# Residual block kernel: first residual sum stored in the output tensor, second sub-layer added to it by accumulating DMAs

## The chip, the cores and the metric

The kernel runs on one core of a Trainium2 chip. The metric is the device time of one execution in microseconds (us), smaller is better. The kernel has five engines at its disposal: TensorE (PE, matrix products; its weight loads are listed as PEld), VectorE (DVE), ScalarE (ACT), GpSimd (POOL) and SyncE (SP). SP only issues transfers here. Transfers that POOL issues go through a queue of their own, which the profile calls software_dynamic; those of SP go through one called hardware_dynamic. Both queues are served by the same 16 DMA engines.

## The reference, cut to what matters

One layer over a sequence of 1024 tokens with 1024 channels, all float32. Only the last two lines of the first half and the last line concern the change: `x` after the first sub-layer is read twice, once by the normalisation ahead of the second sub-layer and once more by the final sum.

```
h = rmsnorm(x, pre_mix_g) * (1.0 + sc1) + sh1
y = hybrid_mixer(h, ...)                     # convolution branch + stick-breaking attention, gated, then w_o
x = x + ga1 * rmsnorm(y, post_mix_g)         # first residual sum
h = rmsnorm(x, pre_ffn_g) * (1.0 + sc2) + sh2
y = swiglu_ffn(h, w_ffn_in, w_ffn_out)       # (silu(gate) * up) @ w_ffn_out
return x + ga2 * rmsnorm(y, post_ffn_g)      # second residual sum, the output
```

## The kernel before, in words

Everything is kept transposed: a tile has 128 channels on the partitions and tokens along the row. The 1024 channels are 8 row blocks (`KT`), the 1024 tokens are two halves `c` of 512 (`CH`). The output in memory is `out[8, 128, 1024]`: row block, channel, token.

The kernel goes through the mixer, then the projection `w_o` with the first residual sum, then the first product of the second sub-layer (22 steps `f`, results stored to `g_d`), then the second product of the sub-layer (block from L1540 on). Each product of two float32 matrices is made of three passes with a high and a low part, and the larger ones are cut into seven block products instead of eight (Strassen's scheme), whose results are called `c11`, `c12`, `c21`, `c22`: the first digit is the half of the channels (row blocks 0 to 3 or 4 to 7) and the second the half of the tokens.

**First residual sum.** `res_add(c, n)` (L921) adds the block of `x` to the normalised `w_o` result on VectorE (L923), then stores the sum with a GpSimd transfer (`store`, helper L107) to a scratch tensor `x1_d[n]` in device memory (L924), then squares it on ScalarE for the next normalisation. There are 16 such stores, 128 rows of 2 KB each.

**Second product.** Three sweeps over 11 steps (`sweep`, names pa, pb, pc; matmuls at L1500), each step with weights that SP loads (`w2f` from `w_d`, helper L104), and then a last loop of 11 steps for the seventh block product, done in two halves of 256 tokens so that the first half can be finished while the second is multiplied. While it runs, `sum_sq` and `finish(1, 0)` finish tokens 512 to 1023; then, after the first half, `finish(0, 0)` finishes tokens 0 to 255; after the very last matmul, `finish(0, 1)` finishes tokens 256 to 511.

**finish(c, h, ps_sum, yy, last)** (L1624). From the channel sums of squares in PSUM it makes the reciprocal root (`rstd_from`: two ScalarE operations at L151 and L152, three on VectorE at L153 to L155). Then for four pairs `m` of row blocks: two multiplies by the reciprocal root (L1637 where the gain has been applied already, L1640 where it is applied in the same instruction), two adds of the first residual sum (the helper `add`, L1540 in the profile), and one store of the pair to `out` by SP (`load` is used for it, so that its line is L104). The pair is 128 partitions by two rows of 512 tokens (512 KB) for `c = 1` and by two rows of 256 tokens (256 KB) for each half of `c = 0`. That makes 12 stores.

**load_x1(c, alloc)** (L1647) brings the first residual sum back: eight transfers of 256 KB by SP for each half of the tokens, 16 in all, from `x1_d` into tiles `xr`: for `c = 1` into the pool `px` (four buffers, which the tiles of `c11` use before), for `c = 0` into four buffers of the pool `ops`, tag `op`, that the tiles `X` have used before.

**What sets the order.** Each engine and each queue executes its instructions in order. The framework's planner picks that order: it simulates the program with its own costs and takes, by priority, what is ready, so that transfers are issued well ahead of the loop in which they stand and the multiplies and adds of `finish` are not interleaved as they are written. Semaphores are set by the framework from the tiles that instructions share; `tc.add_manual_dep` adds an edge by hand.

Of the kernel before, what the change touches and what calls it, by code (L numbers as in the profile page):

```python
# [10 lines left out]
F32 = mybir.dt.float32  # L11
# [3 lines left out]
ALU = mybir.AluOpType  # L15
# [3 lines left out]
P = 128  # L19
D = 1024  # L20
T = 1024
KT = D // P
CH = 512
# [52 lines left out]
def tile_block(ctx: ExitStack, tc: tile.TileContext, xT, vecs, ada1, ada2, win, wv, wcv, wat, wo, w1, w2, cvw, out):  # L76
    nc = tc.nc
    act, dve, pool, pe = nc.scalar, nc.vector, nc.gpsimd, nc.tensor
# [6 lines left out]
    hp = mkpool(ctx, "hp", 16)  # L85
    dp = ctx.enter_context(tc.tile_pool(name="dp", bufs=1, space=DRAM))

    x1_d = [dp.tile([P, T], F32, name=f"x1_d{k}") for k in range(KT)]
    o_d = [dp.tile([P, T], F32, name=f"o_d{k}") for k in range(4)]
    v_d = [dp.tile([NG, P, TM], F32, name=f"v_d{k}") for k in range(CONVT)]  # L90
    u_d = [dp.tile([NG, P, TM], F32, name=f"u_d{k}") for k in range(CONVT)]
# [11 lines left out]
    def load(dst, src):  # L103
        return nc.sync.dma_start(dst, src)  # L104

    def store(dst, src):
        nc.gpsimd.dma_start(dst, src)  # L107
# [42 lines left out]
    def rstd_from(dst, m, a, ps_sum, n):  # L150
        act.activation(dst, ps_sum, AF.Abs_reciprocal_sqrt, bias=eps, scale=1.0 / n)  # L151
        act.activation(m, ps_sum, AF.Identity, bias=eps, scale=1.0 / n)  # L152
        dve.tensor_tensor(a, dst, dst, op=ALU.mult)  # L153
        dve.scalar_tensor_tensor(a, m, -0.5, a, op0=ALU.mult, op1=ALU.mult)
        dve.scalar_tensor_tensor(dst, a, 1.5, dst, op0=ALU.add, op1=ALU.mult)  # L155
# [47 lines left out]
    def bank(name):  # L203
        return psm.tile([P, CH], F32, tag="main", name=name)
# [428 lines left out]
    with ExitStack() as sG:  # L633
# [28 lines left out]
        for j in range(HK):  # L662
            f = [pg.tile([P, T], F32, tag="f", name=f"f{q}_{j}", bufs=2) for q in range(2)]
# [147 lines left out]
        for n in range(KT):  # L811
# [5 lines left out]
            y = yc[n]  # L817
# [35 lines left out]
    with ExitStack() as sF:  # L853
# [53 lines left out]
            pe.matmul(ps_sum, ones, src, start=True, stop=True)  # L907
            return ps_sum

        xrt = {}  # L910

        def xr_load(c):
            for n in range(0, KT, 2):
# [7 lines left out]
        def res_add(c, n):  # L921
            y, xr = h2[n, c], xrt[c, n // 2][:, n % 2]
            dve.tensor_tensor(y, y, xr, op=ALU.add)  # L923
            store(x1_d[n][:, c * CH:(c + 1) * CH], y)  # L924
            act.activation(xr, y, AF.Square)

        pairs_w = {}
# [193 lines left out]
        def a(n):  # L1121
            res_add(0, n)
# [96 lines left out]
        def a(n):  # L1219
            res_add(1, n)  # L1220
# [244 lines left out]
    with ExitStack() as sG:  # L1465
# [39 lines left out]
        def pull(n):  # L1505
            while todo and len(ahead) < n:
                fn, j = todo.popleft()
                ahead.append(fn(j))
# [30 lines left out]
        def add(eng, o, a, b):  # L1539
            eng.tensor_tensor(o, a, b, op=ALU.add)  # L1540
# [57 lines left out]
        def prep4(j, w):  # L1598
            return (wop2 if j < 6 else op2)(f"wa22_{j}", w[:, 0], act, dve)
# [5 lines left out]
        def out_tiles(nm, alloc):  # L1605
            for m in range(2):
                ytile[nm, m] = alloc[m](f"y{nm}_{m}")
            return [ytile[nm, n // 2][:, n % 2] for n in range(NH)]

        def sq_tile(name):  # L1610
            return po_.tile([P, CH], F32, tag="wt", name=name, bufs=3)

        def sum_sq(name, ys):
            acc = pg.tile([P, CH], F32, tag="acc", name=name, bufs=2)
            for n, y in enumerate(ys):
                if n == 0:
                    act.activation(acc, y, AF.Square)
                else:
                    sq = sq_tile(f"{name}_{n}")
                    act.activation(sq, y, AF.Square)  # L1620
                    add(dve, acc, acc, sq)
            return acc

        def finish(c, h, ps_sum, yy, last=None):  # L1624
            n = ps_sum.shape[-1]
            cols = slice(h * n, (h + 1) * n)
            dcols = slice(c * CH + h * n, c * CH + (h + 1) * n)
            rs = pg.tile([P, CH], F32, tag="rs", name=f"frs{c}{h}", bufs=2)[:, :n]
            m, a = (sq_tile(f"frs{c}{h}{i}")[:, :n] for i in "ma")
            rstd_from(rs, m, a, ps_sum, D)  # L1630
            for m in range(4):
                xr = xrs[c, m]
                y = ytile[yy[m // 2], m % 2]
                for i in range(2):
                    yi = y[:, i, cols]
                    if c == 0 and m < 2:
                        dve.tensor_tensor(yi, yi, rs, op=ALU.mult)  # L1637
                    else:
                        src = last[2 * (m - 2) + i][:, cols] if last else yi
                        dve.scalar_tensor_tensor(yi, src, gpost2[:, 2 * m + i:2 * m + i + 1], rs, op0=ALU.mult,  # L1640
                                                 op1=ALU.mult)
                    add(dve, yi, yi, xr[:, i, cols])
                load(out[2 * m:2 * m + 2, :, dcols].rearrange("n p t -> p n t"), y[:, :, cols])

        xrs = {}

        def load_x1(c, alloc):  # L1647
            for m in range(4):
                t = alloc(f"xr{c}_{m}")
                for i in range(2):  # L1650
                    load(t[:, i], x1_d[2 * m + i][:, c * CH:(c + 1) * CH])
                xrs[c, m] = t

        c11_d = dp.tile([P, NH, CH], F32, name="c11_d")
        c12 = out_tiles("c12", (h_tile, h_tile))
# [25 lines left out]
        def mmh(dst, h, n, j, w):  # L1681
            mm(dst, w, [t[:, h * W:(h + 1) * W] for t in T4[j]], n, False, j == FH - 1, True)

        A22 = []
        for j in range(FH):
            pull(1 + AHEAD)
            A22.append(prep4(j, ahead.popleft()))
            if j == FIN_AT[0]:
                load_x1(1, x_tile)
                ps1 = bank("fsum1")  # L1690
                pe.matmul(ps1, ones, sum_sq("acc1", c12 + c22), start=True, stop=True)
            if j == FIN_AT[1]:
                finish(1, 0, ps1, ("c12", "c22"))
            for n in range(NH):
                mmh(ka[n][:, :W], 0, n, j, A22[j])
        load_x1(0, g_tile)
        out_tiles("c11", (g_tile, g_tile))
        for m in range(2):
            load(ytile["c11", m], c11_d[:, 2 * m:2 * m + 2])
            for i in range(2):  # L1700
                y = ytile["c11", m][:, i]
                act.activation(y, y, AF.Copy, scale=gpost2[:, 2 * m + i:2 * m + i + 1])
        c21 = out_tiles("c21", (h_tile, h_tile))
        for h in range(2):
            cols = slice(h * W, (h + 1) * W)
            if h:
                for n in range(NH):
                    for j in range(FH):
                        mmh(ka[n][:, W:], 1, n, j, A22[j])
            ps0 = bank(f"fsum0{h}")[:, :W]  # L1710
            pe.matmul(ps0, ones, acc0[:, cols], start=True, stop=False)
            for n in range(NH):
                sq = sq_tile(f"fsq{h}_{n}")[:, :W]
                y = ka[n][:, cols]
                if h == 0:
                    y = c21[n][:, cols]
                    act.activation(y, ka[n][:, cols], AF.Copy)
                act.activation(sq, y, AF.Square)
                pe.matmul(ps0, ones, sq, start=False, stop=n == NH - 1)
            finish(0, h, ps0, ("c11", "c21"), ka if h else None)  # L1720
# [70 lines left out]
```

## Time and profile before

| | us |
|---|---|
| runs | 1421.28, 1414.62, 1413.15 |
| median | 1414.62 |
| span of the profiled execution | 1415.0 |
| PE busy in it | 1383.6 |
| DVE busy | 1060.4 |
| ACT busy | 651.3 |
| POOL busy | 96.7 |

The span is the time from the first to the last instruction of the one execution that the profiler recorded; it lies 0.4 us over the median of the runs. "Busy" is the time in which an engine executed something; issuing a transfer isn't counted. In the views below a row of a window gives its length, then for each engine its busy time with the number of instructions, then the TensorE clock granted (1 is full speed), the busy share of the 16 DMA engines and the GB/s moved. A row of the timeline gives start, duration, engine, line, operation and the tiles written and read. The chain of waits is the path that ended last, followed back from the end.

### The profile page before, as it was taken

Reading aid. Unit: us, or ns where it says so; the run is one execution under the profiler, and the core shown is the slowest. Engines: PE = TensorE matmul, PEld = TensorE weight load, DVE = VectorE, ACT = ScalarE, POOL = GpSimd, SP = SyncE. Lnnn points to the kernel's source line nnn. Section 1 sums busy time; section 2 is a strip of 40 time slices with the busy share of each in tenths; the row PEclk is TensorE's granted clock in tenths of the full one; section 3 lists DMA queues with packets and bytes.
Section 4 is the critical chain, followed back from the end, with each engine's and each line's share of the span. In section 5 each row is a group of like instructions: output and inputs, shape, how many; then the busy total and the mean of one; then the engine's idle time right before and its main releaser. Section 6 shows DMA issues by size and latency. Waiting matters only on the chain.

```text
span 1415.0 us, 18809 instructions
## 1 busy us (share of the span) xinstructions
PE 1383.6 (98%) x6886; PEld 1156.1 (82%) x6886; DVE 1060.4 (75%) x1602; ACT 651.3 (46%) x1136; POOL 96.7 (7%) x183
## 2 busy tenths in 40 slices
PE   7999999999999999999999999999999999999996
PEld 4798898898888878888877778888888887888886
DVE  6898598576767789779588878778877775775357
ACT  5375465364553447412356553334444453334441
POOL 0000000000001110000012100001111110000000
PEclk8999999999999999999999999999999999999998
DMA  9112041131253645784935545456777769588833
GB/s 382 74 37 75 30 141 54 45 114 66 77 177 111 228 179 175 280 277 137 361 120 173 185 147 173 157 173 228 242 255 246 259 245 392 170 333 280 281 116 119
DMA packets 91116, 258.73 MB, mean 183 GB/s; under 512 B 9744, under 2 KB 20112, under 8 KB 90000
## 3 DMA queue, kind: packets, MB, share of 16 engines
q1 hardware_dynamic: 75088, 202.99, 42.1%
q0 software_dynamic: 15936, 54.54, 10.3%
q8 instruction: 54, 0.88, 0.3%
q14 instruction: 38, 0.31, 0.1%
HBM read 190.91 MB, written 66.58 MB: 182 GB/s over the span
## 4 chain that ended last, share of the span: by engine, by line
PE 80%; DVE 6%; issue 6%; DMA 5%; ACT 2%; POOL 1%; SPq 0%; DVEq 0%; POOLq 0%; ACTq 0%
PE ka L958 12%; PE ka L1500 8%; PE kc L958 7%; PE pwo L881 6%; PE pb L1500 4%; PE pgv L180 3%; PE pg L180 3%; PE pyc L180 3%; PE pya L180 3%; PE pv L481 3%; PE pcv L461 3%; PE tr L571 2%; PE pq L180 2%; PE pgg L180 2%; PE pk L180 2%
## 5 line engine op out<-in xcount | busy, mean ns | idle before, releaser
L559 DVE TENSOR_TENSOR_SCAN ka<-ka 128x128 f32<-128x128 f32 (+2 forms) x96 | 91.4, 968 | 22.8 <-ACT ka L555 22.5
L555 ACT ACTIVATE ka<-z 128x128 f32<-128x128 f32 (+2 forms) x96 | 47.1, 496 | 58.8 <-PE z L554 34.4
L575 DVE TENSOR_TENSOR alo<-tr,ahi 128x512 fp32r<-128x512 f32 x80 | 53.2, 685 | 18.2 <-ACT ahi L574 17.5
L1500 PE MATMUL ka<-gt,w2f 128*128 128x512 f32 x264 | 63.4, 390 | 0.8 <-DMA w2f<-w_d 0.8
L574 ACT ACTIVATE ahi<-tr 128x512 fp32r<-128x512 f32 x80 | 46.3, 601 | 38.1 <-PE tr L571 25.8
L561 DVE TENSOR_TENSOR be<-be,ka 128x127 f32<-128x127 f32 (+2 forms) x96 | 53.4, 573 | 9.6 <-ACT be L556 4.9
L1500 PEld LDWEIGHTS ka<-gt,w2f 128*128 128x128 f32 x264 | 49.4, 188 | 11.5 <-issue 1.4
L1066 PE MATMUL ke<-b,w_hi 128*128 128x512 f32 x176 | 55.2, 394 | 0.0
L135 DVE SCALAR_TENSOR_TENSOR ada<-ada,cb 128x1024 f32<-128x1024 f32 x32 | 38.8, 1223 | 20.7 <-DMA ada<-in_ada_dram 20.6
L556 ACT ACTIVATE be<-z 128x128 f32<-128x128 f32 (+2 forms) x96 | 46.2, 495 | 9.5 <-PE tr L571 9.3
L571 PE MATMUL tr<-ident,be 128*128 128x128 f32 x288 | 47.8, 273 | 0.4 <-DVE alo L575 0.4
L580 PE MATMUL av<-ahi,vst 128*128 128x256 f32 x160 | 44.2, 292 | 0.0
L461 PE MATMUL pcv<-ph,cvw 128*128 128x128 f32 x320 | 42.5, 276 | 0.8 <-DMA ph<-v_d 0.8
L581 PE MATMUL av<-alo,vst 128*128 128x256 f32 x160 | 42.8, 293 | 0.0
L461 PEld LDWEIGHTS pcv<-ph,cvw 128*128 128x128 f32 x320 | 39.5, 192 | 1.5 <-issue 1.2
L1066 PEld LDWEIGHTS ke<-b,w_hi 128*128 128x128 f32 x176 | 33.0, 188 | 7.8 <-issue 1.0
L481 PE MATMUL pv<-wv_hi,hhi 128*128 128x256 f32 x128 | 36.8, 288 | 2.1 <-DVE qst L505 1.4
L159 ACT ACTIVATE gt<-X 128x512 fp32r<-128x512 f32 x33 | 20.4, 630 | 39.5 <-DVE X L1543 12.4
L481 PE MATMUL pv<-wv_hi,hlo 128*128 128x256 f32 x128 | 36.7, 287 | 0.0
L481 PE MATMUL pv<-wv_lo,hhi 128*128 128x256 f32 x128 | 36.4, 285 | 0.0
L551 PE MATMUL z<-kst,qst 128*128 128x256 f32 (+2 forms) x96 | 36.2, 382 | 0.0
L571 PEld LDWEIGHTS tr<-ident,be 128*128 128x128 f32 x288 | 34.7, 140 | 1.8 <-PE z L554 0.5
(533 smaller groups left out, 4097.7 us busy)
## 6 DMA issues: line engine op xcount, KB each, us to landing
w_d<-w2o POOLq DMA_DIRECT2D x44, 512.0 KB, 8.0
w2f<-w_d SPq DMA_DIRECT2D x44, 512.0 KB, 5.4
ada<-in_ada_dram SPq DMA_DIRECT2D x32, 512.0 KB, 6.1
w2r<-in_w_dram SPq DMA_DIRECT2D x44, 256.0 KB, 3.8
w1g<-in_w_dram SPq DMA_DIRECT2D x21, 512.0 KB, 3.6
w1u<-in_w_dram SPq DMA_DIRECT2D x21, 512.0 KB, 5.2
cvw<-in_cvw_dram SPq DMA_DIRECT2D x20, 512.0 KB, 3.7
ada_w<-in_ada_dram SPq DMA_DIRECT2D x8, 1024.0 KB, 12.0
```

The source lines that it names most:

```text
L180: pe.matmul(bank, st[:, cols], mv[k][:, c * CH:(c + 1) * CH], start=(i == 0 and s == 0), stop=(i == n - 1 and s == 2))
L461: pe.matmul(cv[:, gi * TM:(gi + 1) * TM], wts[n][:, at:at + P], ph[:, g, SH - 1 - d:SH - 1 - d + TM], start=(d == 0), stop=(d == SH - 1))
L481: pe.matmul(pv[:, :256], st[k][:, tcols], mv[:, wc], start=(k == 0 and i == 0), stop=(k == KT - 1 and i == 2))
L555: act.activation(kap[:, s_lo:s_hi], z[:, zo:zo + w], AF.Sigmoid, bias=0.0, scale=-0.125)
L559: dve.tensor_tensor_scan(rev, rev, rev, init, op0=ALU.mult, op1=ALU.bypass)
L561: dve.tensor_tensor(beta[:, :m], beta[:, :m], kap[:, s_lo + 1:s_lo + 1 + m], op=ALU.mult)
L571: pe.transpose(tr[:, o:o + P], src, ident)
L575: dve.tensor_tensor(alo, tr, ahi, op=ALU.subtract)
L881: pe.matmul(bank_, st[:, cols], mv[k][:, cs], start=(k == 0 and q == 0), stop=(k == KT - 1 and q == 2))
L958: pe.matmul(bank_, st[:, cols], t[:, mv], start=(first and j == 0 and s == 0), stop=(j == HK - 1 and s == 2), skip_group_check=not first)
L1066: pe.matmul(kbs[f], wes[f][st][:, cols], t[:, mv], start=(i == 0 and j == 0 and q == 0), stop=(j == HK - 1 and q == 2), skip_group_check=i ...
L1500: pe.matmul(dst, w[st][:, cols], g[mv], start=first and s == 0, stop=last and s == 2, skip_group_check=more)
```

## The change

The scratch tensor `x1_d` is gone. `res_add` stores the first residual sum into `out`, at the place of the final result, still with a GpSimd transfer, and keeps a handle on it. `finish` no longer adds on VectorE; each pair of scaled row blocks is sent to `out` by a GpSimd transfer with `accum_op=ALU.add`, which adds to what lies in memory. By hand, each of the 12 accumulating transfers is made to depend on the two stores that wrote its place. `load_x1`, its two calls and the tiles `xr` of this block are gone.

```
-    x1_d = [dp.tile([P, T], F32, name=f"x1_d{k}") for k in range(KT)]
...
-        xrt = {}
+        xrt, x1_st = {}, {}
...
         def res_add(c, n):
             y, xr = h2[n, c], xrt[c, n // 2][:, n % 2]
             dve.tensor_tensor(y, y, xr, op=ALU.add)
-            store(x1_d[n][:, c * CH:(c + 1) * CH], y)
+            x1_st[c, n] = nc.gpsimd.dma_start(out[n, :, c * CH:(c + 1) * CH], y)
             act.activation(xr, y, AF.Square)
...
             for m in range(4):
-                xr = xrs[c, m]
                 y = ytile[yy[m // 2], m % 2]
                 for i in range(2):
                     yi = y[:, i, cols]
...
                         dve.scalar_tensor_tensor(yi, src, gpost2[:, 2 * m + i:2 * m + i + 1], rs, op0=ALU.mult,
                                                  op1=ALU.mult)
-                    add(dve, yi, yi, xr[:, i, cols])
-                load(out[2 * m:2 * m + 2, :, dcols].rearrange("n p t -> p n t"), y[:, :, cols])
-
-        xrs = {}
-
-        def load_x1(c, alloc):
-            for m in range(4):
-                t = alloc(f"xr{c}_{m}")
+                acc = nc.gpsimd.dma_start(out[2 * m:2 * m + 2, :, dcols].rearrange("n p t -> p n t"),
+                                          y[:, :, cols], accum_op=ALU.add)
                 for i in range(2):
-                    load(t[:, i], x1_d[2 * m + i][:, c * CH:(c + 1) * CH])
-                xrs[c, m] = t
+                    tc.add_manual_dep(acc.ins, x1_st[c, 2 * m + i].ins.name,
+                                      mybir.DependencyInfo(mybir.DependencyClass.Sync, mybir.DependencyReason.DATA))
...
             if j == FIN_AT[0]:
-                load_x1(1, x_tile)
...
-        load_x1(0, g_tile)
```

## The prediction

> **What bounds the kernel now.** I read the page first, then the windows of the last stage, then the chain of waits at its end. The page says who is full:
>
> ```profile
> span 1415.0 us, 18809 instructions
> PE 1383.6 (98%) x6886; PEld 1156.1 (82%) x6886; DVE 1060.4 (75%) x1602; ACT 651.3 (46%) x1136; POOL 96.7 (7%) x183
> PE   7999999999999999999999999999999999999996
> ```
>
> PE is busy for 1383.6 of 1415.0 us; the slices show the rest at the two ends. DVE is busy for 75%, but what it does beside a full PE costs nothing. So I ask of each edit whether it sits where PE has run dry. The windows of the second product, and what PE waits for in them (window 1200 to 1420):
>
> ```profile
> 1200.00:1250.00 50.00, 50.00 (x222) 41.40 (x222) 37.11 (x59) 21.72 (x39) 0.00 (x0) 1.00 0.57 192
> 1250.00:1300.00 50.00, 49.25 (x217) 40.26 (x216) 33.84 (x54) 12.98 (x22) 0.00 (x0) 1.00 0.93 349
> 1300.00:1350.00 50.00, 50.00 (x222) 41.42 (x221) 20.34 (x30) 24.75 (x42) 0.00 (x0) 1.00 0.77 256
> 1350.00:1380.00 30.00, 30.00 (x181) 26.60 (x180) 18.02 (x28) 14.15 (x23) 0.00 (x0) 1.00 0.31 100
> 1380.00:1390.00 10.00, 10.00 (x78) 9.71 (x77) 9.65 (x15) 3.35 (x10) 0.00 (x0) 1.00 0.00 1
> 1390.00:1402.00 12.00, 12.00 (x101) 11.97 (x100) 9.52 (x24) 1.89 (x5) 0.00 (x0) 1.00 0.73 263
> 1402.00:1415.00 13.00, 1.83 (x9) 1.27 (x8) 6.96 (x19) 1.22 (x3) 0.00 (x0) 0.68 0.24 81
> ...
> PE ka L1500 <- DMA w2f<-w_d: 0.8, 1, 0.8
> ```
>
> The first number after the length is PE's busy time. It equals the length everywhere but in two rows: 0.75 us are missing between 1250 and 1300, the one wait of PE, for a weight; and PE does 1.83 of the last 13 us. Only these two places can give time. The chain of waits of the last one:
>
> ```profile
> 1402.10 1.74 PE fsum L1719 x8
> ...
> 1403.87 0.48 ACT frs L151
> ...
> 1405.83 1.43 DVE yc L1637 x4
> 1407.26 1.57 DVE yc L1640 x4
> 1408.83 0.33 DVE yc L1540
> 1409.16 0.34 DVEq L1786
> 1409.50 2.01 DVE yc L1540 x6
> ```
>
> After the last matmul come the reciprocal root (to 1405.83), eight multiplies (to 1408.83), eight adds (to 1411.51) and the last store. The planner has put all multiplies ahead of all adds.
>
> **The change part by part.**
>
> *First sums stored to `out`.* 16 GpSimd stores before, 16 after, same tiles and row lengths, on the same queue. Zero; they lie around 718 to 776, beside a PE that has other work.
>
> *16 loads of the first sum, gone.* They are on SP's queue, between the weights. The chain of waits at the one gap of PE:
>
> ```profile
> 1245.82 0.44 SPq L104
> ...
> 1246.80 8.66 DMA xr<-x_d
> ...
> 1255.52 10.40 DMA w2f<-w_d
> 1265.92 0.14 issue
> 1266.05 2.99 PE ka L1500 x12
> ```
>
> By this chain it is the landing of an `xr` load, after 8.66 us, that lets SP go on at 1255.5, and the weight that it issues then lands 10.40 us later, in a window whose DMA engines are 0.93 busy. Without the eight loads of `c = 1` (2 MB) that weight comes earlier by more than 0.75 us, so the wait goes: -0.75 us, at most. The least it can be is zero, if the planner fills the room with other early loads. I take -0.75. Next to be late is nothing that the rows show: every other row of the stage is full. The eight loads of `c = 0` lie in 1300 to 1350, where PE waits for nothing: zero.
>
> *24 adds, gone.* Three groups of eight on DVE:
>
> ```profile
> 1382.42 5.39 DVE L1640 SCALAR_TENSOR_TENSOR yc<-yc,gpost,frs 128x512 f32<-128x512 f32 x8
> 1387.73 4.90 DVE L1540 TENSOR_TENSOR yc<-yc,xr 128x512 f32<-128x512 f32 x8
> ...
> 1396.93 2.77 DVE L1540 TENSOR_TENSOR yc<-yc,xr 128x256 f32<-128x256 f32 x8
> ```
>
> The first 4.90 and the second 2.77 us run under PE: zero. The last eight, from 1408.83 to 1411.51, are on the path: the last transfer's data are ready 2.68 us earlier.
>
> *12 stores by SP become 12 accumulating transfers by POOL.* What is behind them on POOL: nothing, its last record in the trace is a store at 1185.88. Each also waits for two stores of the first sums, which were issued some 600 us before: zero. What they cost is the way to the first byte, the data and the landing. Before:
>
> ```profile
> 1185.88 0.54 POOL L107 DMA_DIRECT2D g_d<-p  x1 [0.78 <-DVE p L1394]
> ...
> 1409.53 2.38 SPq L104 DMA_DIRECT2D out_dram<-yc  x4
> ...
> 1409.53:1410.30 0.77, 0.00 (x0) 0.00 (x0) 0.77 (x3) 0.00 (x0) 0.00 (x0) 0.50 0.00 0
> 1410.30:1413.80 3.50, 0.00 (x0) 0.00 (x0) 1.21 (x4) 0.00 (x0) 0.00 (x0) 0.50 0.87 300
> 1413.80:1415.00 1.20, 0.00 (x0) 0.00 (x0) 0.00 (x0) 0.00 (x0) 0.00 (x0) 0.50 0.00 0
> ```
>
> SP issues the first of the last four at 1409.53 and no byte moves for 0.77 us; then the 16 engines are busy for 0.87 x 3.50 = 3.05 us with the megabyte; 1.20 us after it the span ends. For POOL the nearest rows are the stores of the first sums around 718: the whole group by line, landing times in the window 715 to 735, and the windows behind the first issue, which started at 718.36:
>
> ```profile
> L107 POOL DMA_DIRECT2D x_d<-y x16 | 8.7, 542 | 143.1 <-DVE y L923 142.9
> ...
> x_d<-y POOLq DMA_DIRECT2D x8, 256.0 KB, 2.3
> ...
> 718.36:719.10 0.74, 0.74 (x5) 0.62 (x4) 0.74 (x2) 0.36 (x1) 0.54 (x1) 1.00 0.00 0
> 719.10:719.40 0.30, 0.30 (x3) 0.23 (x2) 0.30 (x2) 0.10 (x1) 0.00 (x0) 1.00 0.00 0
> 719.40:719.70 0.30, 0.30 (x3) 0.26 (x2) 0.30 (x1) 0.30 (x1) 0.14 (x1) 1.00 0.91 355
> ```
>
> An issue takes POOL 0.54 us, the first byte moves 1.04 us after its start, and 256 KB land after 2.3 us. An accumulate has 256 rows where these have 128, so an issue may take up to 1.08 us. The pairs become ready at 1406.55, 1407.26, 1408.04 and 1408.83, about 0.76 us apart; at 1.08 us each the last issue would start at 1406.55 + 3 x 1.08 = 1409.79. That is before the data of the earlier ones are through in what follows, so it costs nothing.
>
> The unknown is how long the data of an accumulate occupy the engines: call it k times the 3.05 us of a megabyte's plain store. Below, k = 1: the add is free. Then the last issue decides, 1408.83 + 2.3 = 1411.13, and with 1.20 us behind it the span would end at 1412.3, 2.7 us earlier. That is the gain's limit. Above there is no row; but an accumulate must read the old megabyte as well as write the new one, which before was a load and a store, so k = 2 is what the bytes ask for if nothing is overlapped. I take k = 2, the nearest to rows of this kernel: data from 1406.55 + 1.04 = 1407.59 for 6.1 us to 1413.69, and 1.20 us to the end at 1414.9. Against 1415.0 that is -0.1 us: what the adds give, the second reading takes.
>
> The Trainium skill (Collectives: The Full Stack, section The bandwidth ceiling: the fold count and why AG ≠ RS ≠ AR) has the add itself as free and says that its cost is the second source read on the same ring, 32.35 against 62.28 GB/s. By that, 1.93 x 3.05 = 5.9 us, an end at 1414.7 as an estimate from that page; no run here shows it yet.
>
> *Sum.* 1415.0 - 0.75 - 0.1 = 1414.15 for the profiled execution. Its span stands 0.4 us over the median of the runs, so 1413.8 us. With k = 1 it is 1412.3 - 0.75 - 0.4 = 1411.15.
>
> **The rivals.** About 0.5% of this kernel, 7.1 us, is what a measurement can tell from no change.
>
> *Slower: the accumulates back up.* The twelve move 4 MB, 12.2 us of plain data, and the first pair is ready after two of the eight multiplies at 1382.42, at 1383.77, its first byte moves at 1384.8. If k is large, the engines never run dry from there and the end is 1384.8 + 12.2 k + 1.2. This passes the forecast's way of reckoning at k = 2.5; k = 3 gives 1422.6, less 0.75 and 0.4 is 1421.4; k = 4 gives 1433.6. From about k = 3 on it is over 0.5% slower. For it: rows of 1 KB and 2 KB, each with a read, a read and a write, and nothing in the trace that shows such a transfer. Against: the plain store of the same rows runs at 300 GB/s in its window, and k = 3 asks for more than the bytes do.
>
> *Each accumulate waits for the one before to land,* if the framework sees one tensor written twice. A landing is 2.3 us and another 0.76 of data: 1406.55 + 4 x 3.06 + 1.20 = 1420.0, less 0.75 and 0.4 is 1418.8. With landings over 3.8 us it would pass 0.5%. Against: the 12 stores before go to the same tensor and four were issued within 2.38 us.
>
> *The adds weren't what ended last, or the change frees more than I see.* The multiplies would end at 1408.83 in any case; to be faster by 7.1 us over half of the 13 us behind the last matmul would have to go, or a gap of PE that the windows don't show. No row speaks for it, except that the planner orders the stage anew.
>
> **How the numbers follow.** Forecast, k from 1 to 2.5: 0.70, at 1411 to 1416. k from 2.5 to 3: 0.06, up to 1421, still within 0.5%. k over 3: 0.15, slower. One after the other: 0.05, of which 0.03 within 0.5% and 0.02 slower. Faster by an order that I don't see: 0.04. So faster 0.04, same 0.70 + 0.06 + 0.03 = 0.79, slower 0.15 + 0.02 = 0.17. The range goes from 1411, the free add, to 1425, k = 3.3, which leaves out about 0.16 in all.
>
> **What would show it.** Right: no `xr` load in the second product, the wait at 1266 gone, PE full until its last matmul about 0.75 us earlier; the first of the last four accumulates issued by POOL some 0.8 us after the first multiply of `finish(0, 1)` starts; about 6 us of busy DMA engines behind it. Step by step wrong: an issue over 1.1 us on POOL (the issue would bound the tail), busy DMA engines without a break from 1385 to the end (backlog), POOL waiting for a transfer between accumulates (one after the other), a new wait of PE in the sweeps (the planner). A time under 1407.5 or over 1421.7 would make the forecast wrong.

## The result, and the profile after

The changed kernel took 1420.12 us in the median of ten runs (1417.39 to 1423.29), the kernel before 1414.49 us in the ten runs beside them: a ratio of 1.0032, 95% interval 1.002 to 1.0045. By this ratio it became slower by some 4.5 us (the two medians lie 5.6 us apart, within the interval's 2.8 to 6.4). No change was forecast, with a time 0.8 us under the median then known. The difference lies within the 0.5% that was called no change, but it is clear of the noise and has the other sign.

The profiled execution after the change has a span of 1416.8 us. First the page, then the windows of the second product that answer to those of before (same columns: PE, PEld, DVE, ACT, POOL, clock, DMA share, GB/s):

```profile
span 1416.8 us, 18768 instructions
PE 1383.9 (98%) x6886; PEld 1157.1 (82%) x6886; DVE 1051.1 (74%) x1578; ACT 651.2 (46%) x1136; POOL 111.0 (8%) x195
```
```profile
1250.00:1300.00 50.00, 50.00 (x222) 41.39 (x222) 32.05 (x51) 14.49 (x25) 0.00 (x0) 1.00 0.81 288
1300.00:1350.00 50.00, 50.00 (x222) 41.40 (x221) 20.12 (x30) 22.08 (x38) 0.00 (x0) 1.00 0.68 223
...
1380.00:1390.00 10.00, 10.00 (x76) 9.68 (x76) 6.74 (x14) 2.92 (x9) 4.82 (x4) 1.00 0.84 130
1390.00:1402.00 12.00, 10.33 (x80) 9.77 (x78) 2.86 (x8) 1.99 (x5) 4.83 (x4) 1.00 0.93 155
1402.00:1417.00 15.00, 0.00 (x0) 0.00 (x0) 3.29 (x9) 0.00 (x0) 4.86 (x4) 0.52 0.53 70
```

PE is full from 1250 on, the gap at 1266 is gone, and it is through with its work before 1402. Two numbers from here on measure every kernel: the **sweeps**, from the first matmul of the second product to the end of the last matmul of all, and the **tail**, from there to the end of the span. The start of the sweeps is the first start time in the next two rows (this line's matmuls, before and after), the end is the last matmul's row in the timeline (1398.44 + 1.89 = 1400.33; before, 1403.83):

```profile
L1500 PE MATMUL ka<-gb,wa x132: 389/389/497, 1186.1 to 1243.1; 128*128 128x512 f32 x132
```
```profile
L1499 PE MATMUL ka<-gb,wa x132: 389/389/499, 1183.7 to 1240.8; 128*128 128x512 f32 x132
```
```profile
1398.44 1.89 PE L1709 MATMUL fsum<-fsq,ones 128*128 128x256 f32 x8
```

The sweeps went from 217.7 to 216.6 us, 1.1 us less. The tail went from 11.2 to 16.5 us, 5.3 us more. The sum, +4.2 us, is what the runs show; that the sweeps begin 2.4 us earlier in this execution is left out of it, since in the executions of the kernels below they begin anywhere from 1183.7 to 1189.7.

Where the tail went: the accumulates on POOL and the last multiplies in the timeline, the transfers of the window 1404 to 1417, and the windows in which the last megabyte moves and after it.

```profile
1402.33 1.43 DVE L1635 TENSOR_TENSOR yc<-yc,frs 128x256 f32<-128x256 f32 x4
1403.39 4.86 POOL L1640 DMA_DIRECT2D out_dram<-yc  x4 [8.40 <-DVE yc L1635]
1403.68 1.65 DVE L1638 SCALAR_TENSOR_TENSOR yc<-ka,gpost,frs 128x256 f32<-128x256 f32 x4
```
```profile
DMA packets 1088, 1.05 MB, mean 81 GB/s; under 512 B 64, under 2 KB 1088, under 8 KB 1088
...
q0 software_dynamic: 1088, 1.05, 61.5%
...
out_dram<-yc POOLq DMA_DIRECT2D x4, 256.0 KB, 6.2
```
```profile
1404.90:1412.90 8.00, 0.00 (x0) 0.00 (x0) 0.43 (x2) 0.00 (x0) 3.35 (x3) 0.50 1.00 131
1412.90:1416.80 3.90, 0.00 (x0) 0.00 (x0) 0.00 (x0) 0.00 (x0) 0.00 (x0) 0.50 0.00 0
```

The adds are gone, and the data are ready at 1405.3. But the 16 DMA engines are full for 8.0 us (61.5% of 13 us) with the megabyte that took them 3.05 us, and when the last byte has moved, at 1412.8, there are 4.0 us in which no engine computes and no byte moves. Before there were 1.4. What the second stretch is, the waits of SP at the very end tell, before and after:

```profile
SPq L1786 <- DMA out_dram<-yc: 1.7, 3, 0.7
SPq L1786 <- PEq L1786: 0.6, 2, 0.5
```
```profile
SPq L1776 <- DMA out_dram<-yc: 43.6, 2, 42.3
SPq L1776 <- PEq L1776: 2.9, 2, 2.5
```

The first row of each is the wait for the output to land. The second is the closing barrier, where all engines meet: SP stood there for up to 2.5 us instead of 0.5. The page's name PEq is only who came last by its reckoning. The records of the trace themselves (start in us, duration, engine, operation) name the one who was late:

```
after    1405.60  10.43  GpSimd  DRAIN
         1405.62   2.62  GpSimd  DMA_DIRECT2D out_dram<-yc   (the last accumulate)
         1413.76   0.01  Sync    DRAIN                        (SP is at the barrier)
         1416.08   0.02  GpSimd  EVENT_SEMAPHORE              (GpSimd is at the barrier)
before   1185.86   8.43  GpSimd  DRAIN
         1185.88   0.54  GpSimd  DMA_DIRECT2D g_d<-p          (its last transfer)
         1414.29   0.01  Sync    DRAIN
         1414.32   0.02  GpSimd  EVENT_SEMAPHORE
```

The last instruction of GpSimd's own program is a drain. Before, it began at 1186 and nobody saw it. Now it begins behind the last accumulate and ends 3.2 us after the last byte, 2.3 us after SP has seen everything land.

### The profile page after: what moved, and what is told of

It is laid out like the page before. It is cut to its first block, busy times and chain, and to the rows that moved or that the text cites. A ratio compares the mean times of both kernels' runs of the same rounds, so it can differ in the third digit from the quotient of the medians.

```text
span 1416.8 us, 18768 instructions
## 1 busy us (share of the span) xinstructions
PE 1383.9 (98%) x6886; PEld 1157.1 (82%) x6886; DVE 1051.1 (74%) x1578; ACT 651.2 (46%) x1136; POOL 111.0 (8%) x195
## 4 chain that ended last, share of the span: by engine, by line
PE 87%; issue 4%; DVE 3%; DMA 2%; ACT 2%; POOL 1%; POOLq 0%; SPq 0%; DVEq 0%; ACTq 0%
PE ka L957 14%; PE kc L957 8%; PE ka L1499 8%; PE pwo L880 6%; PE pb L1499 4%; PE pgv L179 3%; PE pyc L179 3%; PE pg L179 3%; PE pya L179 3%; PE pv L480 3%; PE pcv L460 3%; PE ka L414 2%; PE tr L570 2%; PE pq L179 2%; PE pgg L179 2%
## 5 line engine op out<-in xcount | busy, mean ns | idle before, releaser
L158 ACT ACTIVATE s1o<-s 128x512 fp32r<-128x512 f32 x22 | 13.8, 629 | 49.7 <-PE ka L957 41.6
```

## The experiments

Two theories were set against each other: A, that the end is tied to GpSimd's drain, and B, that it is tied to the longer data time of the accumulates. A table first; the numbers of each row are from the profiled execution of that kernel, the ratio is to the kernel before on the same chip. "Last byte" is counted from the end of the last matmul, "behind it" from there to the end of the span.

| kernel | sweeps | last byte | behind it | tail | ratio (95%) |
|---|---|---|---|---|---|
| before | 217.7 | 9.8 | 1.4 | 11.2 | 1 |
| after | 216.6 | 12.5 | 4.0 | 16.5 | 1.0032 (1.002 to 1.0045) |
| e1_plain_pool | 216.6 | 8.0 | 4.6 | 12.6 | 1.001 (0.9996 to 1.0024) |
| e2_sp_no_add | 216.6 | 6.9 | 1.4 | 8.3 | 0.9973 (0.996 to 0.9985) |
| e3_one_pool_store | 217.5 | 10.2 | 4.2 | 14.4 | 1.0035 (1.0022 to 1.0048) |
| e4_half | 217.3 | 9.8 | 1.7 | 11.5 | 0.9996 (0.9983 to 1.0008) |
| e6_three_quarters | 216.9 | 10.2 | 1.4 | 11.6 | 1.0001 (0.9989 to 1.0012) |
| e7_split_adds | 216.6 | 10.8 | 2.5 | 13.3 | 1.0016 (1.0004 to 1.0028) |
| e8_tiny_pool | 217.4 | 10.0 | 4.2 | 14.2 | 1.0025 (1.0007 to 1.0043) |
| e9_loads_on_pool | 216.6 | 10.4 | 2.5 | 12.9 | 1.001 (0.9995 to 1.0024) |
| e10_loads_only | 216.6 | 9.8 | 1.4 | 11.2 | 1.0002 (0.9989 to 1.0015) |
| e11_tiny_compute | 217.8 | 9.8 | 3.8 | 13.5 | 1.0014 (1.0 to 1.0028) |

**e1_plain_pool.** From the changed kernel, with the scratch tensor back:

```
-                acc = nc.gpsimd.dma_start(out[...], y[:, :, cols], accum_op=ALU.add)
+                store(out[...], y[:, :, cols])
```

> The changed kernel with plain GpSimd stores in place of the accumulating ones (the first residual sum is left out of the output). Theory A: the end is set by GpSimd's closing drain, which in the changed kernel ends 7.8 us after the end of the last transfer's issue on that engine. Then the end stays tied to that issue: the stretch from the last matmul's end to the end of the span is 14.0 us (if a plain issue takes 0.54 us) to 16.5 us (if it takes 1.2 us), where the changed kernel has 16.5 and the kernel before 11.2. Rival B: the longer data time of the accumulates (7.3 us for the last megabyte against 3.05) sets it. Then the stretch falls to 8.6 us: multiplies, a landing of 2.5 us and the closing.

```profile
1407.60 2.96 POOL L107 DMA_DIRECT2D out_dram<-yc  x4 [10.39 <-DVE yc L1636]
```
```profile
DMA packets 321, 1.06 MB, mean 92 GB/s; under 512 B 64, under 2 KB 64, under 8 KB 320
...
q0 software_dynamic: 320, 1.05, 26.7%
...
out_dram<-yc POOLq DMA_DIRECT2D x4, 256.0 KB, 2.9
```

The first fence is the timeline of POOL, the second the transfers from 1406.5 to 1418. Neither theory got its number: 12.6 us of tail lies between 8.6 and 14.0. The drain ended 5.8 us behind the last issue, not 7.8, so A in its first form fell; but it ended 3.8 us behind the last byte, where the changed kernel has 3.2. Both costs are real then. From e2_sp_no_add to this kernel the queue alone is exchanged: 4.3 us more tail, 1.1 until the last byte and 3.1 behind it. From this kernel to the changed one the add alone is put in: 3.9 us more, 4.5 until the last byte and 0.6 less behind it. The plain store goes out in 256 packets of 4 KB beside 64 small ones (320 in all), the accumulate in 1024 of 1 KB, one for each row (1088). But the number of packets doesn't explain the longer time: SP's plain store of the same rows, in the kernel before, also takes 1024 of 1 KB, and its 27.8% of 11 us are the 3.05 us again (window 1404 to 1415):

```profile
DMA packets 1088, 1.05 MB, mean 95 GB/s; under 512 B 64, under 2 KB 1088, under 8 KB 1088
...
q1 hardware_dynamic: 1088, 1.05, 27.8%
```

By the packets' records a 1 KB packet takes 102 ns in the median when it accumulates and 46 ns in SP's plain store; a 4 KB packet of GpSimd's plain store takes 187.

**e2_sp_no_add.** From the kernel before: no `load_x1`, no add, the stores by SP behind the multiplies.

```
-                    add(dve, yi, yi, xr[:, i, cols])
...
-                load_x1(1, x_tile)
...
-        load_x1(0, g_tile)
```

> The kernel before without the 24 adds and the 16 loads, stores by SP right behind the multiplies (the first residual sum is left out of the output). Both theories: this is the gain with nothing paid for it. Stretch behind the last matmul 11.2 - 2.7 = 8.5 us, PE's last matmul about 1.1 us earlier counted from the first matmul of the second product, together some 3.8 us faster than before, ratio 0.9973.

As expected within 0.2 us: sweeps 216.6, tail 8.3 us, ratio 0.9973. So the two savings that the change aims at are there, 1.1 us in the sweeps and 2.9 in the tail. What remains is the price.

**e3_one_pool_store.** The kernel before, one store moved:

```
-                load(out[...], y[:, :, cols])
+                (store if c == 0 and h == 1 and m == 3 else load)(out[...], y[:, :, cols])
```

> The kernel before, with only its very last output store issued by GpSimd and not by SP. Theory A: the closing drain of GpSimd now starts behind that store: issue from 1411.5, 0.54 to 1.2 us, 7.8 us of drain, 0.75 us of closing, so the stretch behind the last matmul grows from 11.2 to 16.8 to 17.4 us and the time by 5.6 to 6.2 us, ratio 1.004. Rival B: a plain store costs at most 0.5 us more on GpSimd's queue, ratio 1.000.

One plain transfer of 256 KB on the other queue makes the tail 3.2 us longer, and the kernel slower clear of the noise; the interval of its ratio, 3.1 to 6.8 us, holds the tail's 3.2 us at its lower end. SP's waits at the end:

```profile
SPq L1786 <- PEq L1786: 3.2, 2, 2.7
SPq L1786 <- DMA out_dram<-yc: 3.0, 1, 3.0
```

Rival B has no room for that. The 5.6 to 6.2 us of A were too many, again because the drain follows the last byte (by 3.4 us) and not the issue.

**e4_half.** `c = 1` accumulates as in the change; `c = 0` loads, adds and stores by SP:

```
+                    if not c:
                        add(dve, yi, yi, xr[:, i, cols])
...
-                load_x1(1, x_tile)
```

> Accumulating transfers only for tokens 512 to 1023, which are finished 20 us before the end; tokens 0 to 511 as before (loads, adds, stores by SP). Theory A: the drain on GpSimd ends at about 1394 and is hidden; stretch behind the last matmul 11.2 us as before, the wait in the sweeps gone (-1.1 us): ratio 0.999. Rival B: the two megabytes of accumulates take about 13 us of the DMA engines from 1381 on and end at 1395, so they may hold up the stores of the next quarter, not the last: -1.1 to 0 us.

Four accumulates that end 17 us ahead of the end cost nothing: tail 11.5, ratio 0.9996, no difference. The drain ended at 1399.9, 3.0 us behind its queue's last byte and unseen. The sweeps gained only 0.4 of the 1.1 us. A wait of 0.4 us for a weight is left in them, which ends at 1264.42; the eight loads that stayed are issued from 1303 on, so they didn't stand in that weight's way:

```profile
PE pb L1503 <- DMA w2f<-w_d: 0.4, 1, 0.4
...
1256.27 8.11 DMA w2f<-w_d
1264.38 0.04 issue
1264.42 3.06 PE pb L1503 x12
...
1303.39 0.79 SPq L104 DMA_DIRECT2D xr<-x_d  x2
```

What made that weight late is open. The transfers of 1383 to 1397, where POOL's queue has these four alone:

```profile
q0 software_dynamic: 1088, 2.10, 89.5%
```

2.1 MB in 1088 packets, 89.5% of 14 us: 6.3 us for a megabyte with rows of 2 KB, 2.1 times a plain store, where the last megabyte of the changed kernel, in rows of 1 KB, takes 2.6 times.

**e6_three_quarters.** Only the last quarter (tokens 256 to 511) as before, the rest accumulates:

```
+                late = c == 0 and h == 1
...
+                    if late:
+                        add(dve, yi, yi, xrs[c, m][:, i])
```

> Accumulating transfers for tokens 512 to 1023 and 0 to 255; only the last quarter, tokens 256 to 511, is loaded back (1 MB and not 4), added on VectorE and stored by SP as before. Theory A, mended: GpSimd's closing drain ends 3.0 to 3.8 us behind the last byte of GpSimd's own queue, whenever that is. Here that byte moves at about 1401 of 1414, so the drain is hidden: tail behind the last matmul 11.2 us, sweeps 216.6 us as without any load (217.7 before): -1.1 us, ratio 0.9992. Rival B (accumulates as such delay the end): their 3 MB end by 1401, the last stores start at 1408, so the same. Both fall if the tail is over 12 us.

The expected 1.1 us came down to 0.4 (sweeps -0.8, tail +0.4), and the runs show no difference. Eight accumulates out of twelve are free as long as the last ones are not among them. One of VectorE's root operations started 0.48 us behind the one before it, where the kernel before has 0.11, which makes the longer tail; the same stands in e7_split_adds, and why is open.

**e7_split_adds.** As e6_three_quarters, with `add(dve if i else pool, ...)`: four of the last eight adds on GpSimd.

> As e6_three_quarters, and four of the eight adds of the last quarter on GpSimd (0.69 us each by the 2759 ns of its 128x1024 subtract, scaled) beside the multiplies. If the eight adds on VectorE are what ends last, the tail falls from 11.2 to about 9.9 us and the whole by 2.4 us, ratio 0.9983. Rival: GpSimd and VectorE hold each other up at their shared memory port, or an add on GpSimd takes longer than scaled; tail 11.2 or more.

```profile
1404.99 1.96 DVE L1641 TENSOR_TENSOR yc<-yc,frs 128x256 f32<-128x256 f32 x4
1406.87 1.65 DVE L1644 SCALAR_TENSOR_TENSOR yc<-ka,gpost,frs 128x256 f32<-128x256 f32 x4
1408.44 1.83 DVE L1544 TENSOR_TENSOR yc<-yc,xr 128x256 f32<-128x256 f32 x4
```

The rival held, and a second cost came on top. VectorE's four plain multiplies took 1.96 us instead of 1.43 and its four adds 1.83 where half of 2.76 would be 1.38. In each four it is a single operation that ran longer, 0.95 and 0.82 us instead of 0.42, and each ended 0.3 us after the GpSimd add that was running when it started. The four multiplies with the gain (L1644) took their 1.65 us as before, beside GpSimd's adds too. With the wait of e6_three_quarters on top, the last add ended 7.7 us after the last matmul, as before. And GpSimd's drain took until 6.1 us after its last add, though its queue had moved its last byte 6 us before that add ended. Slower, 1.0016.

**e8_tiny_pool.** The kernel before, with one transfer more:

```
+                if c == 0 and h == 1 and m == 3:
+                    store(x1_d[0][:, :1], y[:, 1, cols][:, :1])
```

> The kernel before with one more transfer on GpSimd behind the last add: 128 values of 4 bytes to scratch memory; nothing else is changed. Theory A, mended: its last byte moves about 1.1 us after its issue at 1411.5, the drain ends 3.3 us later, 0.77 us of closing: tail 12.9 instead of 11.2 us, ratio 1.0012. Rival C, the drain waits for the transfers of all queues: SP's last byte + 3.3 + 0.77, tail 13.8 us. Rival D, a late transfer on GpSimd costs only its own data: tail 11.2 us.

512 bytes cost 3.0 us of tail; rival D fell. The tail, 14.2 us, is nearer to C's 13.8 than to the 12.9 of the mended A, since these bytes were through 2.0 us after their issue and not 1.1, when SP's last ones were. The drain ended 3.4 us behind them. This kernel can't part A and C, as the two queues end 0.2 us apart; the kernel before does: its drain ended at 1194.3, with SP's queue at work for 200 us more. C fell by that.

**e9_loads_on_pool.** The kernel before with `load_x1` on the other queue, and the adds split as above:

```
-                    load(t[:, i], x1_d[2 * m + i][:, c * CH:(c + 1) * CH])
+                    nc.gpsimd.dma_start(t[:, i], x1_d[2 * m + i][:, c * CH:(c + 1) * CH])
```

> No accumulating transfer at all: the kernel before with its 16 loads of the first residual sum issued by GpSimd, where nothing else is queued after 1186, and four of the eight last adds on GpSimd. If the sweeps lose 1.1 us because the loads stand in SP's queue, they take 216.6 us here; if it is the 4 MB on the DMA engines, 217.7 us. Tail as e7_split_adds, 9.9 us. Ratio 0.9983 or 0.9991.

Sweeps 216.6 us with all 4 MB still loaded: it was the place in SP's queue that cost 1.1 us, not the bytes. The tail was 12.9, not 9.9, much as in e7_split_adds (13.3) and with the same 6.1 us from the last add to the end of the drain.

**e10_loads_only.** As e9_loads_on_pool, all adds on VectorE.

> The kernel before with its 16 loads of the first residual sum issued by GpSimd, and nothing else: no accumulating transfer, adds on VectorE, stores by SP. Sweeps 216.6 us as in e9_loads_on_pool (217.7 before), GpSimd's last transfer at about 1313 so that its drain is hidden, tail 11.2 us as before: -1.1 us, ratio 0.9992. If the tail is longer, something else than late work of GpSimd made it so in e9_loads_on_pool.

Sweeps 216.6, tail 11.2, each as expected. The runs show 1.0002 (0.9989 to 1.0015): a gain of 1.1 us lies within that interval and isn't shown by the times. By sweeps and tail it is the best version with the full output here, 227.8 us together against 228.9 before and 233.1 after the change. Its time can't be told from that of the kernel before; that it is faster than the changed kernel, the two intervals show, which don't overlap.

**e11_tiny_compute.** The kernel before with one small computation on GpSimd and no transfer:

```
+                if c == 0 and h == 1 and m == 3:
+                    pool.tensor_copy(late, y[:, 1, cols][:, :1])
```

> The kernel before with one copy of 128 x 1 values on GpSimd behind the last add, and no transfer there. Theory A, widened: the closing drain costs 6.1 us behind a late computation too, as in e7_split_adds and e9_loads_on_pool: copy at about 1411.6, drain to 1417.9, 0.77 us of closing, tail 14.8 instead of 11.2 us, ratio 1.0025. Rival: the drain waits for transfers alone, and those of GpSimd ended 200 us before: tail 11.2 to 11.6 us, ratio 1.000.

```profile
1410.85 0.18 POOL L1645 COPY late<-yc 128x1 f32<-128x1 f32 x1 [225.21 <-DVE yc L1540]
```
```profile
SPq L1789 <- PEq L1789: 3.0, 2, 2.5
SPq L1789 <- DMA out_dram<-yc: 1.8, 3, 0.7
```

A copy of 0.18 us costs 2.3 us of tail; the interval of the ratio, 1.0 to 1.0028, holds that and starts at no change. The drain lasted until 4.8 us after it, not 6.1, so the expected 14.8 was too much, but the rival, that the drain waits for transfers alone, fell: there were none for 225 us. What the drain does in that time no run shows.

## Why the prediction was wrong, point by point

**The step that failed** is the last term of the tail: "and 1.20 us to the end". It was read from the kernel before, where SP ends the work, and carried over to a kernel where GpSimd does (1.20 us is the window from 1413.80 on; from the last byte, at 1413.6, it was 1.4). It measured 4.0 us from the last byte, 2.6 more than before on the same footing. e3_one_pool_store, e8_tiny_pool and e11_tiny_compute each show it with next to nothing else changed. The prediction asked what is queued behind the accumulates on POOL and answered "nothing, its last record in the trace is a store at 1185.88". It looked at records that count as busy. A drain stood behind that store, for 8.43 us.

**k, the data of an accumulate**, was taken as 2 by the bytes and measured 2.6 in the tail (8.0 against 3.05 us): 1.9 us mis-sized. Elsewhere 2 was near. The accumulates of `c = 1`, with rows of 2 KB, took 2.1 times a plain store (e4_half), and those of tokens 0 to 255, with the same rows of 1 KB as the last ones, 2.2 times. In the changed kernel's window 1395 to 1400 these have the engines to themselves:

```profile
DMA packets 889, 0.85 MB, mean 169 GB/s; under 512 B 64, under 2 KB 889, under 8 KB 889
...
q0 software_dynamic: 889, 0.85, 107.5%
```

107.5% of 5 us for 0.85 MB make 6.6 us for 1.05 MB. (The share passes 100% where the records of neighbouring packets overlap.) So the length of the rows doesn't make the 2.6. The packets' records show what is different in the last megabyte: the median of a 1 KB packet is 102 ns in both, but 75 of the 1024 took over 150 ns, up to 1.19 us, where there were 2 such among those of tokens 0 to 255. 70% of that excess lies before 1408.24, while GpSimd was still issuing. That the issues held these packets up is argued, not shown; no run varied it. The Trainium skill (Collectives: The Full Stack, section The bandwidth ceiling: the fold count and why AG ≠ RS ≠ AR) puts the cost of an add at the second source read, 1.93 times; the trace agrees roughly for the transfers of `c = 1` and of tokens 0 to 255 (2.1 and 2.2 times) and differs in the last megabyte (2.6 times), where the measurement decides.

With k at 2.6 the prediction's own sum would have come to 1407.59 + 7.9 + 1.2, less 0.75 and 0.4, some 1415.5 us. That is 0.9 us over the median then known, where some 4.5 were measured, so the wrong k alone doesn't explain the result.

**The first byte** moved 1.75 us after the first accumulate's issue (1403.39 to 1405.14) where 1.04 was taken from a store of 128 rows. An issue took 1.2 us when alone, and up to 2.7 by its record when the next came before it was done; the four together took 4.86 us, 1.2 each. That is over the 1.08 of the forecast and over the 1.1 us which it named as a sign that the issue would bound the tail. The last issue was done at 1408.24, 4.6 us ahead of the last byte, so it isn't what ended last; whether it slowed the data before that is the open point above.

**The readiness of the first pair** came 3.06 us after the last matmul, 0.3 us later than reckoned. Together: 0.3 + 0.7 + 1.6 + 2.8 = 5.4 us from the forecast's tail of 11.1 to the measured 16.5, where 1.6 is the data (7.7 us from first to last byte, not 6.1) and 2.8 the end.

**The loads.** The wait at 1266 went, as predicted; the sweeps became 1.1 us shorter, where 0.75 was forecast. The other 0.4 us is busy time of PE, which ran the same 1078 matmuls in 216.6 us instead of 217.0. The bytes don't matter: with all 4 MB moved by GpSimd's queue the sweeps take 216.6 us too (e9_loads_on_pool, e10_loads_only). That the loads of `c = 0` are free, as the prediction has it, isn't settled: e4_half and e6_three_quarters, which keep eight loads in SP's queue (half as long in the second), stay 0.7 and 0.3 us over 216.6, but e7_split_adds has the same loads as e6_three_quarters and takes 216.6, and in e4_half the wait comes ahead of the loads.

**The adds**: 2.7 us forecast for the path, 2.9 measured (e2_sp_no_add). Right.

**The base.** "Its span stands 0.4 us over the median of the runs" was taken as the offset between span and time. In all runs of all kernels here the time is 1.7 to 1.8 us over the span of the same execution, so the profiled execution of before was one of its longer ones. The forecast is the median plus the changes and isn't moved by that, but single spans of two kernels can't be compared to 2 us; that is why sweeps and tail are compared here.

**The rivals.** The backlog didn't come: no byte of an accumulate moves from 1400.5 to 1405.1, so the first eight were through. Nor did the accumulates wait for one another: four issues lie within 2.2 us. The slower outcome came by a mechanism that none of the rivals named. The measured 1420.1 us lies inside the stated range only by luck: the part of it above 1416 was put there for a backlog, or a chain of accumulates, that didn't come. And in the second rival the landing that would pass 0.5% is 3.0 us, not 3.8; 3.8 is that landing with the 0.76 us of data.

## What to carry to other kernels

Ask which engine does the last work, and what its program still has to do when that work is done: a saving of 2.9 us on VectorE's last adds was paid for with 5.6 us more until the last byte (12.5 against 6.9 without any add) and 2.6 us of GpSimd's closing drain, because the last transfers had become accumulates of GpSimd. GpSimd's transfers, accumulating ones too, cost nothing that the runs show where their last byte moved 11 us ahead of the end (e6_three_quarters); nothing between that and the end itself was tried. And when a profile says that an engine is idle behind its last instruction, look at what it does until the barrier, not only at what counts as busy.

## What the runs showed of the hardware that was not expected

- GpSimd's closing drain ends 3.0 to 3.8 us after the last byte of its own queue, in nine kernels of this case whose last work on GpSimd is a transfer, whether 512 bytes or a megabyte, plain or accumulating, store or load, and whether other queues still move. Behind a late computation it takes 4.8 us (one copy of 128 values) to 6.1 us (adds of 128x256). From the end of the drain to the end of the span it is another 0.8 us where GpSimd is the last.
- An accumulating transfer from on-chip memory to device memory goes out in one packet for each row, like SP's plain store of these rows, while a plain one of GpSimd's queue goes out in packets of 4 KB. In the median a 1 KB packet takes 102 ns accumulating and 46 plain, a 2 KB one 178 and 84, and a 4 KB plain one 169 to 187 ns.
- The issue of an accumulating transfer takes GpSimd 1.2 us for 256 rows, where a plain one takes 0.72 us for 256 rows and 0.54 for 128.
- A plain multiply or add of VectorE that starts while GpSimd adds (0.72 to 0.78 us for 128x256) takes 0.82 to 0.98 us instead of 0.42 and ends 0.3 us after GpSimd's add, in e7_split_adds and e9_loads_on_pool; VectorE's multiplies with the gain, whose source is the matmul's result `ka`, keep their 0.47 us beside it.
